# A residual stream with the model dimension on partitions, in a two-layer hybrid attention trunk

## The chip, the cores and the metric

The kernel runs on one core of one Trainium2 chip. The metric is device time in microseconds of one execution, as the median of several runs. A core has a matrix engine (TensorE, PE in the profile; PEld is its loading of weights), a vector engine (VectorE, DVE), a scalar engine (ScalarE, ACT), GpSimd (POOL) and SyncE (SP), which here only issues transfers. Each engine takes its instructions in order and waits on semaphores for the others. On-chip memory (SBUF) and the accumulators that TensorE writes (PSUM) both have 128 partitions. Transfers between SBUF and main memory (HBM) run on 16 DMA engines.

## What is computed

Two layers over x, 2048 tokens of model dimension 1024, in float32:

```python
def rms_norm(x, g):
    y = x * rsqrt(mean(x * x, axis=-1, keepdims=True) + 1e-6)
    return y * g

def even_layer(x, ...):                    # layer 0
    proj = rms_norm(x, norm_g) @ w_in      # aq, ak, av, ag, bq, bk, bv, bg
    aq, ak: rms_norm per head of 64, then rotary;  bq, bk: rms_norm per head
    ya = sliding_window_sink_attention(aq, ak, av, sinks) * silu(ag)
    yb = chunked_relbias_attention(bq, bk, bv, rel) * silu(bg)
    return x + concatenate([ya, yb]) @ w_out

def odd_layer(x, ...):                     # layer 1
    q, k, v, gate = split(rms_norm(x, norm_g) @ w_in)     # 1024 columns each
    q, k: rms_norm per head of 64, then rotary
    o = differential_attention(q1, q2, k1, k2, v, lam)    # 8 heads, values 128 wide
    return x + (rms_norm(o, subln_g) * (1 - lambda_init) * silu(gate)) @ w_out
```

## The kernel before

**Layout and precision.** Tokens are handled in four blocks (`BLK` = 512 tokens, `NB` = 4) of four tiles of 128 (`NTB`); the model dimension is eight slices (`KT`) of 128. Every float32 operand of a projection is split into a high part H, the value rounded to the type in which TensorE multiplies it fast, and a low part L, the rest. One product is three matmuls, H by H, H by L and L by H (`mm3`, lines 211 to 216). A matmul contracts over partitions, so the normed input must lie with the model dimension on partitions, while x and the residual between the layers (`self.x1`, a scratch tensor [S, D] in HBM) lie with tokens on partitions.

**Four stages.** Tile names begin with the stage: p0 (projections of layer 0), m (its attention and output projection), p1 (projections of layer 1), c (its attention, gates and output projection).

**Projection, `_project`, for both layers.** The blocks go in two halves, 3 and 2, then 1 and 0. For each block `hidden` (lines 316 to 345) takes four token tiles: it loads [128 tokens, 1024], squares and sums it on ScalarE (L325), forms the root with `rstd` (L203 to L208, two steps on ScalarE and four on VectorE), multiplies by root and norm weights on VectorE (L327), transposes eight 128x128 pieces on TensorE into PSUM (L332, tiles p0trh and p1trh), and splits them, H on ScalarE (L336) and L on VectorE (L337). In layer 1 it also stores H and L of blocks 3 to 1 (L343, L344), for the gates later. Then each group of 512 weight columns is loaded and split by `weights_by` (L303, L309 on ScalarE, L311 on GpSimd) and multiplied with both blocks. A tile of a query or key group goes through `normed` (L361 to L378): squares, sums per head, `rstd`, product, rotary on VectorE and GpSimd. After four tiles `pairs_out` (L385 to L396) transposes them and stores H and L. Value groups are copied and stored. Gate groups of layer 0 end in a sigmoid by Exp, Ln, Exp on ScalarE and a product on VectorE (L452 to L455). In layer 1 the groups are two of queries, two of keys, two of values (`cv`, L483).

`later` is a side job: `split_weights` splits weights that are needed later and stores H and L to HBM, in chunks of 512 columns. It is advanced once a group from the third group of a half on (`AHEAD` = 2); layer 1 has four chunks, two of the output weights and two of the gate weights, and they fall to groups three to six of half 0.

**Attention of layer 0, `_mix0`.** Heads go through the blocks from 3 to 0. Beside them run the last gates of the projection (`late_gate`) and, block by block, the output projection (`out_tile`): eight tiles per block, which multiply y (stationary) with the output weights (moving), add x (L505) and store to x1 (L506). Block 0's projection stands alone at the end.

**Attention of layer 1, `_mix1`.** `pace` advances scores and values of the heads, and beside them `gates` (projection of the gate columns, copied at L1088 and stored) and the output projection (`out_begin`, `out_step`, `out_end`).

**Memory.** Pools are stacked in the order in which they are opened, and layer 1's lie where layer 0's were. So the first tiles of p1 wait for the last reader of what lay there. In layer 0 the order is `big` (64 KB a partition: first the hidden blocks, then the output weights, columns 0 to 511 in its first half), `y` (36 KB: the split y), `yt`, then the rest. In layer 1 it is `hv` (32 KB), `ev` (32 KB), weights, then the others; `hidden` puts a half's first block into `ev` and its second into `hv`.

**Order.** The engines' orders are fixed when the program is built, from the order of the calls and what is ready; the calls of `weights` and of `later` alternate, and both take their staging tiles (`ws`, two in layer 1) and their w tiles (28) from the same pools.

## Time and profile before

| what | us |
|---|---|
| median of 3 runs | 2805.61 (2803.16 to 2806.72) |
| the profiled execution | 2808.08 |
| its span in the trace | 2806.3 |
| mean granted TensorE clock | 0.987 of full |
| p0: until its last matmul | 597.7 |
| m: until the end of the output projection | 1164.2 |
| p1: until its last matmul | 1757.4 |
| c: the rest | 1049 |

Rows of the profile name line, engine, operation, the tile written and those read, shapes, and after the bar the busy time, the mean duration in ns, and the engine's idle time just before with what ended it. A row of a stage gives, for a stretch of the span, the busy time and instruction count of each engine, the granted clock, the DMA engines' share and the rate in GB/s. A row of waits gives total, count and longest. "xN" counts instructions. Durations of neighbouring matmuls overlap, so their spacing is read from starts.

### The profile page before, as it was taken

How to read it: one execution, taken by the hardware profiler on the slowest of the kernel's cores; microseconds unless marked ns; L12 is line 12 of the kernel's file. 1: busy time of each engine (PE TensorE's matmuls, PEld its weight loads, DVE VectorE, ACT ScalarE, POOL GpSimd, SP SyncE). 2: the span in 40 equal slices, each digit the busy share in tenths (PEclk: the TensorE clock that was granted, in tenths of full speed). 3: DMA queues.
4: the chain of work that ended last, by engine and by line, in shares of the span. 5: the costliest groups of instructions: out<-in, count | busy, mean ns of one | idle time of the engine just before them, and what ended most of it. 6: DMA issues, size and time to landing. Idle time of an engine off the chain costs nothing.

```text
span 2806.3 us, 44052 instructions
## 1 busy us (share of the span) xinstructions
PE 2697.3 (96%) x13384; PEld 2169.2 (77%) x13384; DVE 1853.8 (66%) x4616; ACT 1606.4 (57%) x4039; POOL 1462.8 (52%) x1551
## 2 busy tenths in 40 slices
PE   7999999999899999899999999999999999999998
PEld 5888888888788888777788888777676777676776
DVE  7762285346777775598808870569886878777762
ACT  5443543367767675334334331578896787777761
POOL 3541252335545454267745670457676666767661
PEclk9999999999999999999999999999999999999999
DMA  5673343738866764666885444787868666454542
GB/s 174 225 242 140 109 142 122 232 109 239 240 179 191 201 192 132 209 217 207 253 256 192 135 136 142 239 256 219 238 190 230 183 212 200 132 183 144 166 146 83
DMA packets 356093, 521.69 MB, mean 186 GB/s; under 512 B 44816, under 2 KB 139792, under 8 KB 355856
## 3 DMA queue, kind: packets, MB, share of 16 engines
q1 hardware_dynamic: 355856, 518.87, 60.2%
q8 instruction: 107, 1.75, 0.3%
q14 instruction: 130, 1.06, 0.1%
HBM read 361.70 MB, written 157.02 MB: 185 GB/s over the span
## 4 chain that ended last, share of the span: by engine, by line
PE 77%; DVE 9%; DMA 6%; ACT 3%; issue 2%; POOL 2%; SPq 1%; DVEq 0%; ACTq 0%; POOLq 0%
PE cO L975 8%; PE p1mm L215 5%; PE p1mm L214 5%; PE p1mm L216 5%; PE cS L919 4%; PE cS L920 4%; PE ctr L971 4%; PE p0mm L214 4%; PE p0mm L216 4%; PE p0mm L215 4%; PE com L214 2%; PE com L215 2%; PE com L216 2%; PE cG L214 2%; PE mom L214 2%
## 5 line engine op out<-in xcount | busy, mean ns | idle before, releaser
L926 ACT ACTIVATE cP<-cS,cnm 128x512 f32<-128x512 f32 (+3 forms) x640 | 394.1, 621 | 138.4 <-DVE cnm L923 121.9
L923 DVE TENSOR_REDUCE cnm<-cS 128x1 f32<-128x512 f32 (+3 forms) x640 | 373.4, 600 | 52.2 <-PE cS L920 45.9
L959 POOL TENSOR_TENSOR cP<-cP,cP 128x512 f32<-128x512 f32 (+1 forms) x320 | 356.4, 1143 | 27.6 <-ACT cP L957 26.7
L958 POOL TENSOR_SCALAR cP<-cP,crl,cel 128x512 f32<-128x512 f32 (+3 forms) x288 | 210.7, 745 | 231.6 <-DVE crl L940 126.5
L214 PE MATMUL p1mm<-p1wH,p1hH 128*128 128x512 f32 x768 | 303.4, 396 | 5.5 <-ACT p1wH L309 5.5
L215 PE MATMUL p1mm<-p1wL,p1hH 128*128 128x512 f32 x768 | 304.4, 397 | 0.1
L216 PE MATMUL p1mm<-p1wH,p1hL 128*128 128x512 f32 x768 | 303.9, 396 | 0.0
L975 PE MATMUL cO<-cpt,cv 128*128 128x512 f32 (+3 forms) x640 | 288.0, 535 | 2.1 <-DVE cpt L973 2.1
L311 POOL TENSOR_TENSOR p0wL<-p0ws,p0wH 128x512 fp32r<-128x512 f32 (+1 forms) x124 | 149.7, 1238 | 267.3 <-ACT p0wH L309 263.3
L919 PE MATMUL cS<-ck,cqd 128*128 128x512 f32 (+3 forms) x640 | 265.3, 418 | 6.6 <-ACT cP L926 6.0
L973 DVE COPY cpt<-ctr 128x512 f32<-128x512 f32 (+1 forms) x320 | 191.0, 604 | 107.3 <-PE ctr L971 104.1
L214 PE MATMUL p0mm<-p0wH,p0hH 128*128 128x512 f32 (+1 forms) x640 | 238.5, 374 | 7.0 <-ACT p0vt L473 4.7
L216 PE MATMUL p0mm<-p0wH,p0hL 128*128 128x512 f32 (+1 forms) x640 | 238.3, 373 | 2.0 <-DVE p0hL L337 1.9
L215 PE MATMUL p0mm<-p0wL,p0hH 128*128 128x512 f32 (+1 forms) x640 | 238.4, 373 | 0.0
L311 POOL TENSOR_TENSOR p1wL<-p1ws,p1wH 128x512 fp32r<-128x512 f32 x128 | 167.2, 1327 | 124.6 <-ACT p1wH L309 118.5
L920 PE MATMUL cS<-ck,cql 128*128 128x512 f32 (+3 forms) x640 | 232.0, 367 | 0.0
L971 PEld LDWEIGHTS ctr<-ident,cP 128*128 128x128 f32 x1088 | 138.7, 142 | 115.4 <-issue 62.3
L957 ACT ACTIVATE cP<-cP,cc 128x512 f32<-128x512 f32 (+1 forms) x320 | 189.2, 651 | 18.2 <-DVE cc L943 17.7
L971 PE MATMUL ctr<-ident,cP 128*128 128x128 f32 x1088 | 177.1, 275 | 1.8 <-POOL cP L959 1.5
L214 PEld LDWEIGHTS p1mm<-p1wH,p1hH 128*128 128x128 f32 x768 | 145.8, 190 | 34.6 <-ACT p1wH L309 5.7
L215 PEld LDWEIGHTS p1mm<-p1wL,p1hH 128*128 128x128 f32 x768 | 145.6, 190 | 29.9 <-POOL p1wL L311 0.9
L216 PEld LDWEIGHTS p1mm<-p1wH,p1hL 128*128 128x128 f32 x768 | 145.8, 190 | 28.9 <-issue 0.2
(301 smaller groups left out, 7046.9 us busy)
## 6 DMA issues: line engine op xcount, KB each, us to landing
p1ws<-in_od_w_in_dram SPq DMA_DIRECT2D x56, 512.0 KB, 4.3
p0ws<-in_ev_w_in_dram SPq DMA_DIRECT2D x48, 512.0 KB, 4.2
ck<-kH SPq DMA_DIRECT2D x144, 128.0 KB, 3.4
ck<-kL SPq DMA_DIRECT2D x144, 128.0 KB, 3.5
cv<-v SPq DMA_DIRECT2D x72, 256.0 KB, 4.0
cqd<-qH SPq DMA_DIRECT2D x128, 128.0 KB, 4.6
cql<-qL SPq DMA_DIRECT2D x128, 128.0 KB, 4.7
cwH<-wgH SPq DMA_DIRECT2D x64, 256.0 KB, 5.1
```

The costliest lines, as they stand in the source:

```text
L214: mm(ps, aH, bH, start=first, stop=False)
L215: mm(ps, aH, bL, start=False, stop=False)
L216: mm(ps, aL, bH, start=False, stop=last)
L311: low.tensor_tensor(l[:, :width], ws[:, k, :width], f32(h[:, :width]), ALU.subtract)
L919: mm(ps, qd[:, m, js], kt[:, :wd], start=True, stop=False)
L920: self.anchor = mm(ps, ql[:, m, js], kt[:, :wd], start=False, stop=True).ins
L923: nc.vector.tensor_reduce(nm[:, m, z:z + 1], ps, AX.X, ALU.max, negate=True)
L926: exp = nc.scalar.activation(chunks[z][:, :wd], ps, AF.Exp, bias=nm[:, m, z:z + 1], accum_out=acc).ins
L958: nc.gpsimd.tensor_scalar(p1, p1, rl[:, 0:1], e1, ALU.mult, ALU.mult)
L959: nc.gpsimd.tensor_tensor(p1, p1, p2, ALU.add)
L971: nc.tensor.transpose(tp[:, (j - j0) * P:(j - j0 + 1) * P], us[j][kt // 4][:, kk:kk + P], self.ident)
L975: mm(O[:, j0 * P:], v, T[:, :wd], start=(kt == 0), stop=(kt == nkt - 1), skip_group_check=True)
```

## The change

1. x is given to the kernel, and taken from it, with the model dimension first: x, x1 and the output are [D, S] in HBM. The transposition of both ends is in the host's layout code.
2. `hidden` loads slices [128 of the model dimension, 512 tokens], multiplies by the norm weight per partition while it splits (H on ScalarE, L on VectorE), and no longer applies the root. No transposes.
3. The root per token is applied behind the projection: in layer 0 the squares are summed over slices on GpSimd (`squares`), in layer 1 they are taken and summed in `out_tile` of layer 0. `roots` sums over partitions with one-column matmuls, forms the root as a column per token tile (`rcol`), eps times the mean square (`ecol`), and by four transposes the root as a row over all partitions (`row`). Queries and keys need only the eps term, since their own norm cancels the root; values are scaled by the column while they are copied; gates are multiplied by the row.
4. `out_tile` and the output projection of layer 1 swap stationary and moving operand.
5. Around it, mostly in layer 1: the first value group comes first, tables are formed behind it; `normed` takes two tiles at a time, with one of the two rotary sums on VectorE; `pairs_out` is called later (`turn`); the first group of half 0 is issued slice by slice over four PSUM tiles (`project_tiles`); half 1 takes block 0 first; `hidden` exchanges `hv` and `ev`, and the pools' order changes; low parts of later weights are formed on VectorE, two chunks in the last group of half 0 and two in the first of half 1; value tiles are stored from ScalarE's queue. In the attention of layer 1 a query is loaded by four transfers instead of eight, and pools are reordered.

```diff
+    def squares(self, layer, b, sq, first):
+        nc, parts = self.nc, list(sq)
+        if first:
+            self.row[layer][b] = self.rows.tile([P, BLK], F32, tag="row", name=f"row{layer}")
+            if len(parts) > 1:
+                nc.gpsimd.tensor_tensor(self.row[layer][b], parts.pop(0), parts.pop(0), ALU.add)
+        for part in parts:
+            nc.gpsimd.tensor_tensor(self.row[layer][b], self.row[layer][b], part, ALU.add)
+
+    def roots(self, layer, b, sm, sb, ptr):
...
+        for j in range(NTB):
+            nc.tensor.matmul(ps[:, j:j + 1], row[:, j * P:(j + 1) * P], f32(self.ones[:, 0:1]), start=True, stop=True)
+        ms = sm.tile([P, NTB], F32, tag="xms", name=n + "ms")
+        nc.vector.tensor_scalar(ms, ps[:, :NTB], 1.0 / D, EPS, ALU.mult, ALU.add)
+        self.rstd(sm, ms, NTB, "x", r)
+        nc.vector.tensor_scalar(e, ms, EPS, None, ALU.mult)
...
+        for j in range(NTB):
+            js = slice(j * P, (j + 1) * P)
+            nc.scalar.activation(wide[:, js], f32(self.ones), AF.Copy, scale=r[:, j:j + 1])
+            nc.tensor.transpose(ps[:, js], wide[:, js], self.ident)
+        nc.scalar.activation(row, ps, AF.Copy)
+        self.col[layer][b] = r, e
...
         def hidden_tile(part, i):
-            pl, tag = (self.big, "w") if layer == 0 else (self.hv, "h") if i else (ev, "v")
+            pl, tag = (self.big, "w") if layer == 0 else (ev, "v") if i else (self.hv, "h")
...
+            values = [("cv", 2048 + 512 * i, 512, dict(c0=512 * i)) for i in range(2)]
+            groups = values[:1] + groups + values[1:]
...
-                    low = nc.vector if first and k else nc.gpsimd
+                    low = nc.vector if k >= 2 - vector else nc.gpsimd
...
         def hidden(b, i, between=()):
...
+            for q in range(4):
+                xt = xp.tile([P, 2, BLK], F32, tag="xt", name=n + "xt")
+                for i in range(2):
+                    k = 2 * q + i
+                    nc.sync.dma_start(xt[:, i, :], x[k * P:(k + 1) * P, tok])
+                    g = self.norm[layer][:, k:k + 1]
+                    nc.scalar.activation(hH[:, k, :], xt[:, i, :], AF.Copy, scale=g)
+                    nc.vector.scalar_tensor_tensor(hL[:, k, :], xt[:, i, :], g, f32(hH[:, k, :]), ALU.mult, ALU.subtract)
+                if layer == 0:
+                    sq = xp.tile([P, 2, BLK], F32, tag="vb", name=n + "xq", bufs=2)
+                    nc.scalar.activation(sq, xt, AF.Square)
+                    self.squares(0, b, (sq[:, 0, :], sq[:, 1, :]), q == 0)
                 next(between, None)
...
+            self.roots(layer, b, sm, sb, ptr)
...
-                wH, wL = weights(c0 + 512 * i, 512, W)
+                wH, wL = weights(c0 + 512 * i, 512, W, 2 * layer)
...
-                if gi >= self.AHEAD:
+                for _ in range(gi >= self.AHEAD if layer == 0 else 2 * ((half, gi) in ((0, 5), (1, 0)))):
                     next(ahead, None)
...
-                            nc.scalar.activation(gt, ps, AF.Exp, scale=-1.0)
-                            nc.scalar.activation(gt, gt, AF.Ln, bias=self.one)
-                            nc.scalar.activation(gt, gt, AF.Exp, scale=-1.0)
-                            nc.vector.tensor_tensor(gt, ps, gt, ALU.mult)
+                            nc.vector.tensor_tensor(gt, ps, self.row[0][b], ALU.mult)
+                            nc.scalar.activation(sg, gt, AF.Exp, scale=-1.0)
+                            nc.scalar.activation(sg, sg, AF.Ln, bias=self.one)
+                            nc.scalar.activation(sg, sg, AF.Exp, scale=-1.0)
+                            nc.gpsimd.tensor_tensor(gt, gt, sg, ALU.mult)
...
+                            nc.scalar.activation(vt, ps, AF.Copy, scale=rc)
+                            nc.scalar.dma_start(s["v"][tok, o["c0"]:o["c0"] + 512], vt)
...
+            self.mm3(ps, w[0][k][c][:, js], w[1][k][c][:, js], *y[k], i == 0, i == KT - 1, self.anchor)
...
+        if (j, c) == (0, 0):
+            self.squares(1, b, (), True)
+            nc.scalar.activation(self.row[1][b], xr, AF.Square)
+        else:
+            sq = sb.tile([P, BLK], F32, tag="xq", name=n + "xq", bufs=1)
+            nc.scalar.activation(sq, xr, AF.Square)
+            self.squares(1, b, (sq,), False)
...
-                    nc.scalar.activation(gt, ps, AF.Copy)
+                    nc.vector.tensor_tensor(gt, ps, self.row[1][b], ALU.mult)
```

More of the change, by code (lines that the diff above doesn't have):

```diff
@@ new lines, in project_tiles @@
+        def project_tiles(h, w, width, outside):
+            pss = [pmm.tile([P, 512], F32, tag="mm", name=n + "mm") for _ in range(NTB)]
+            steps = [(k, j) for k in range(outside) for j in range(NTB)]
+            steps += [(k, j) for j in range(NTB) for k in range(outside, KT)]
+            for k, j in steps:
+                self.mm3(
+                    pss[j][:, :width], h[0][:, k, j * P:(j + 1) * P], h[1][:, k, j * P:(j + 1) * P],
+                    w[0][k][:, :width], w[1][k][:, :width], k == 0, k == KT - 1,
+                )
+                if k == KT - 1:
+                    yield pss[j]
@@ L419, in _project, with turn @@
         ahead = later()
+        turned = []
+        def turn():
+            while turned:
+                pairs_out(*turned.pop(0))
         for half in range(2):
             blocks = (NB - 1 - 2 * half, NB - 2 - 2 * half)
+            if layer == 1 and half == 1:
+                blocks = blocks[::-1]
             ready = None
@@ L424, in _project @@
                 ready = [], []
-                by = weights_by(groups[0][1], groups[0][2], W, *ready, first=True)
+                by = weights_by(groups[0][1], groups[0][2], W, *ready, vector=1)
                 next(by)
@@ L460, in _project @@
                     xs = []
+                    tiles = project_tiles(h[bi], w, width, 4) if layer == half == gi == bi == 0 else None
                     for j in range(NTB):
@@ new lines, in _project, with out_tile @@
+                        if layer == 0:
+                            turn()
+                if not tabs:
+                    tables()
+            turn()
+    def out_tile(self, y, w, j, b, c, xin, xout, sb, pmm, n, tag, order=range(KT), after=None):
+        nc = self.nc
+        js, tok = slice(j * P, (j + 1) * P), slice(b * BLK, (b + 1) * BLK)
+        cs = slice(c * 512 + j * P, c * 512 + (j + 1) * P)
+        xr = sb.tile([P, BLK], F32, tag="xr", name=n + "xr", bufs=2)
+        nc.sync.dma_start(xr, xin[cs, tok])
+        ps = pmm.tile([P, BLK], F32, tag=tag, name=n + "om")
```

233 lines of the change are left out of this document (116 added, 117 removed).

## The prediction

> **What bounds the kernel now.** I read the page first, then busy time by stage, then who waited for whom on TensorE.
>
> ```profile
> span 2806.3 us, 44052 instructions
> ## 1 busy us (share of the span) xinstructions
> PE 2697.3 (96%) x13384; PEld 2169.2 (77%) x13384; DVE 1853.8 (66%) x4616; ACT 1606.4 (57%) x4039; POOL 1462.8 (52%) x1551
> ```
> ```profile
> core 0: us, PE busy (x) PEld busy (x) DVE busy (x) ACT busy (x) POOL busy (x), PEclk, DMA share, GB/s
> 0.00:60.00 60.00, 40.75 (x189) 32.01 (x190) 49.76 (x112) 32.38 (x77) 20.90 (x22) 0.98 0.56 171
> ...
> 0.00:600.00 600.00, 572.58 (x2845) 479.73 (x2845) 317.61 (x696) 261.26 (x591) 208.93 (x203) 1.00 0.51 167
> 600.00:1120.00 520.00, 493.18 (x3073) 432.76 (x3073) 375.65 (x1260) 370.28 (x984) 256.68 (x386) 0.99 0.69 195
> ...
> 1164.00:1758.00 594.00, 576.58 (x2680) 474.41 (x2678) 390.72 (x681) 220.67 (x496) 331.43 (x256) 0.98 0.60 196
> 1758.00:2806.00 1048.00, 1014.33 (x4606) 748.79 (x4605) 757.32 (x1952) 746.86 (x1953) 663.25 (x704) 0.98 0.62 188
> ```
> ```profile
> 1165.00:1275.00 110.00, 98.38 (x455) 80.43 (x456) 102.20 (x185) 49.33 (x119) 62.19 (x48) 0.94 0.62 217
> ```
>
> The reader is to see TensorE busy for 96% of the span, so nearly everything gained must be TensorE work taken away or a gap closed. Gaps are concentrated: the first 60 us (19 us idle) and the opening of the second layer's projections, where VectorE is busy 102 of 110 us and the granted clock falls to 0.94. The rows of single waits name the cause:
>
> ```profile
> PE p0trh L332 <- DVE p0xt L327: 13.7, 3, 13.1
> ...
> PE p1trq L385 <- DVE p1eL L391: 7.2, 3, 2.9
> ...
> PE p1mm L214 <- ACT p1wH L309: 5.5, 1, 5.5
> ```
>
> **Token transposes removed, both layers.** 256 fp32 transposes (tiles p0trh, p1trh) go.
>
> ```profile
> L332 PE MATMUL p1trh<-ident,p1xt 128*128 128x128 f32 x128 | 17.9, 283 | 3.8 <-DVE p1q8u L206 3.5 <-DVE p1xt L327 0.3
> L332 PE MATMUL p0trh<-ident,p0xt 128*128 128x128 f32 x128 | 17.8, 283 | 15.6 <-DVE p0xt L327 13.7 <-DVE p0hL L337 1.9
> ```
> ```profile
> 37.09 1.04 PE L332 MATMUL p0trh<-ident,p0xt 128*128 128x128 f32 x8
> ...
> 1755.13 0.39 PE L215 MATMUL p1mm<-p1wL,p1hH 128*128 128x512 f32 x1
> ...
> 1757.40 0.39 PE L216 MATMUL p1mm<-p1wH,p1hL 128*128 128x512 f32 x1
> ```
>
> From these, dense spacings: ten projection matmuls in 2.27 us, 0.2275 us each; eight transposes in 1.04 us, the last lasting 0.28, so 0.109 us each inside a run. Added are the `roots`: per block four one-column matmuls and four transposes, eight blocks. The nearest row is the removed transpose at 17.8/128 = 0.14 us; 8 x 0.14 = 1.1 us per block, 4.5 us per layer.
>
> **Start of layer 0.** Today's projections in the first 60 us:
>
> ```profile
> 0.00:60.00 60.00, 33.64 (x129) 24.77 (x130) 2.73 (x4) 2.98 (x5) 0.98 0.56 171
> ```
> ```profile
> 6.89 1.15 ACT L309 ACTIVATE p0wH<-p0ws 128x512 fp32r<-128x512 f32 x2 [4.56 <-DMA p0ws<-in_ev_w_in_dram]
> ...
> 8.26 1.06 ACT L325 ACTIVATE p0junk<-p0xt 128x1024 f32<-128x1024 f32 x1 [0.22 <-DMA p0xt<-in_x_dram]
> ```
>
> The first row is tile p0mm alone: 129 matmuls. Afterwards the first token tile needs all eight slices of the block, not one token tile of x, so it starts no earlier: ScalarE must do eight weight copies (8 x 0.575), eight copies of x at about the same price (4.6) and three double squares (3 x 1.06) from 6.9 us on, ending at 19.3; with the low part and three matmuls I put that tile's end at 21 us. From there TensorE can run dense: (60 - 21)/0.2275 = 171 matmuls, less about 18 for pair transposes and roots, plus the tile's 24 make 177, 48 more than now, 10.9 us. ScalarE stays nearly full for the second block, so I take 9 (bounds 4 to 12). In the second half of layer 0, half of the p0trh row (8.9 us) goes and roots (2.2) come: I take 6. Layer 0: **-15** (bounds -8 to -20). The 24 gate products added to GpSimd and its row sums lie in a stage where it is busy 209 of 600 us in all. A qk root now waits for its block's token root; behind it on VectorE queue further tiles' steps, for which TensorE's four PSUM tiles (24 x 0.2275 = 5.5 us of matmuls each) are the cover. What is late next there is the key/value group's chain on VectorE and ScalarE, unchanged.
>
> **Second layer's projections.** From the row 1164 to 1758: 2304 matmuls x 0.2275 = 524 us, 256 pair transposes x 0.109 = 28, together 552 of 594. The other 42 are token transposes (some 12), waits, and half-speed clock behind the waits. What takes VectorE off: squares and per-token root leave `hidden`, the qk root runs once per two tiles, value columns come first, tables move behind them.
>
> ```profile
> L207 DVE TENSOR_TENSOR p1q8u<-p1q8u,p1q8ms 128x8 f32<-128x8 f32 x26 | 22.4, 860 | 0.7
> ...
> 10.20 0.16 DVE L207 TENSOR_TENSOR p0xu<-p0xu,p0xms 128x1 f32<-128x1 f32 x1
> ```
>
> The first row is the window 1165 to 1360: a root step takes 860 ns there, against 160 alone at 10 us, so halving these steps saves more than their width says. The opening wait (5.5 us) goes as well: x copies land in the two slots whose output weights are read out halfway through the last output projection, and weight tiles lie behind the y tiles. What is late next is the matmul itself. I leave 4 us of waits and 4.5 of roots: 42 - 8.5 = 33.5, **-34** with transposes issued before 1164.
>
> [...]
>
> **Later weights: what the quicker stage collides with.** Today four chunks of later weights (`split_weights`) are spread over four groups. Afterwards two go into the last value group of half 0 and two into the first of half 1, each 8 x 24 x 0.2275 = 43.7 us long. Loads of the next group's weights stand behind them, as now:
>
> ```profile
> 1343.21 0.41 SPq L303 DMA_DIRECT2D p1ws<-in_od_w_out_dram  x1
> ...
> 1347.05 0.45 SPq L303 DMA_DIRECT2D p1ws<-in_od_w_in_dram  x1
> ```
> ```profile
> v<-p1v SPq DMA_DIRECT2D x31, 256.0 KB, 3.2
> ...
> hH<-p1hH SPq DMA_DIRECT2D x3, 2048.0 KB, 8.7
> ...
> p1ws<-in_od_w_out_dram SPq DMA_DIRECT2D x8, 512.0 KB, 4.1
> wo1H<-p1wH SPq DMA_DIRECT2D x16, 256.0 KB, 3.2
> ```
> ```profile
> DMA  9999989999999999999996926086479314000230
> ...
> q1 hardware_dynamic: 11715, 10.46, 75.7%
> ```
> ```profile
> 1180.00:1200.00 20.00, 19.68 (x99) 16.10 (x98) 18.32 (x39) 11.20 (x30) 9.58 (x8) 1.00 1.00 374
> ```
>
> The second fence gives the sizes; eight value tiles of 256 KB, or one block of next weights, are 2.1 MB, hH and hL of a block 4.2. The third is 1429 to 1473, the value group with one chunk: DMA is full for 25 us, 10.7 us are free. A chunk is 4 x 512 KB in and 16 x 256 KB out, 6.3 MB. The first group gains a chunk and a block of x1 (2.1 MB): 8.4 MB at 374 GB/s, 22.4 us, 11.7 late. The second holds two chunks, next weights, x1, value stores (2.1 each) and hH and hL, 23.1 MB, 61.8 us, 18.1 late. For 11.2 us of this, the value stores (moved to ScalarE's queue), nobody waits: **+19**. Bounds: 0, if what is queued first covers it; and with all 44.1 MB of both groups (2.1 of it the last k stores) in the way at that value group's own rate, 10.46 MB in 44 us over its share 0.757, 314 GB/s, 140 - 87 = 53.
>
> **Attention of layer 0.** Each of 32 output tiles adds a square on ScalarE, 28 a sum on GpSimd.
>
> ```profile
> L999 POOL TENSOR_TENSOR cot<-cot,cgg 128x512 f32<-128x512 f32 x32 | 41.5, 1297 | 60.7 <-ACT csq L995 50.6 <-DMA cgg<-g 9.9
> ...
> L995 ACT ACTIVATE csq<-cot 128x512 f32<-128x512 f32 x32 | 20.4, 637 | 0.2
> ...
> L1088 ACT ACTIVATE cgt<-cG 128x512 f32<-128x512 f32 x32 | 19.0, 594 | 15.2 <-PE cG L216 12.1 <-DMA p1hH<-hH 3.0
> ...
> L455 DVE TENSOR_TENSOR p0gt<-p0mg,p0gt 128x512 f32<-128x512 f32 x24 | 16.6, 691 | 97.8 <-ACT p0gt L454 97.8
> ```
>
> 28 x 1.3 = 36 us on GpSimd (257 of 520 busy) and 32 x 0.64 = 20 on ScalarE (370 of 520). The square's buffer is single, so a square waits for GpSimd's last sum, and behind it in ScalarE's queue stand the exponentials the score tiles wait for. TensorE idles 27 us here; raised by GpSimd's 14% that is **+4** (bounds 0 and 36, every sum exposed).
>
> **Attention of layer 1.** The 32 gate copies (0.59 us) leave ScalarE; VectorE gains 32 products, at the 0.69 us of L455. 128 query load issues go from SP's queue, bytes unchanged. Both engines are 71% busy: **0** (bounds -4 and +6).
>
> **Sum.** The profiled execution took 2808.08 us (span 2806.3 and 1.8 around it), 2.5 above the median. 2808.1 - 15 - 34 + 19 + 4 = 2782.1, less 2.5: **2780 us**.
>
> **Rivals.** (a) *Later weights stay hidden.* For: 10.7 us are free in that group, and two staged slices of weights can be loaded ahead. Then +19 becomes 0: 2761. (b) *Squares hold ScalarE in layer 0's attention.* If each of 28 waits one sum of 1.3 us and half of the 36 us reaches TensorE, 18 instead of 4: 2794. Against: output tiles come one in 16 us. (c) *DMA saturates in the two value groups*, the mechanism on the other side: price 53 us instead of 19, 2814, slower. It decides from 50 us late, a rate under 44.1 MB/137 us = 321 GB/s; above that and up to 333 GB/s it ends within 0.2% of before. For: the group already reaches share 1.00 with one chunk. Against: without that group's small packets the row 1180 to 1200 reached 374.
> [...]
> (d) *It doesn't do what it says*: 256 transposes go but 32 wide ones and 32 small matmuls come; counted.
>
> **How the numbers follow.** Forecast 0.45, (a) 0.25, (b) 0.08, (c) 0.22, half of it slower and half within 0.2%, about what a measurement of this kernel can tell from no change. Faster: 0.45 + 0.25 + 0.08 = 0.78. The range 2752 to 2808 takes (a) with layer 0 and the waits at their good ends, and (c) to where it equals before; a tenth is left out on each side.
>
> **What would show it.** Right: no trh rows; the first 60 us with some 175 p0mm matmuls; no wait of p1mm at the stage's opening; VectorE well under 90% behind it; p1mm waiting for p1wH at the end of half 0 and one group on, some 10 us each, with DMA share near 1.00. Wrong: those waits absent (a) or over 20 us each (c); TensorE's idle time from 600 to 1120 up by more than 10 us (b); layer 0's first tile ending after 27 us.

## The result and the profile after

After the change the kernel takes 2881.57 us in the median (2877.17 to 2884.66, 4 runs), before it 2806.16 (2803.16 to 2807.89, 4 runs on the same chip): ratio 1.0269, 95% interval 1.0251 to 1.0287, some 75 us slower. The forecast was 2780, with a range of 2752 to 2808.

The head of the page of the changed kernel:

```profile
span 2875.4 us, 43341 instructions
...
PE 2698.1 (94%) x13224; PEld 2164.3 (75%) x13224; DVE 1873.8 (65%) x4520; ACT 1591.8 (55%) x3911; POOL 1495.1 (52%) x1567
```

The transposes are gone, yet TensorE is busy as long as before (2697.3), and its idle time rose from 109 to 177 us. Busy time by stage shows where; the stages are cut at the end of the last p0mg, mom and p1mm matmul. First the kernel before, then the changed one (columns as in the prediction's rows):

```profile
0.00:598.10 598.10, 571.11 (x2834) 478.46 (x2835) 316.56 (x691) 259.43 (x589) 208.12 (x203) 1.00 0.51 167
598.10:1164.30 566.20, 535.63 (x3272) 467.72 (x3270) 389.20 (x1293) 379.48 (x1004) 260.06 (x389) 0.99 0.68 192
1164.30:1757.80 593.50, 576.08 (x2677) 474.07 (x2675) 390.71 (x681) 220.53 (x495) 331.43 (x256) 0.98 0.60 196
1757.80:2806.30 1048.50, 1014.53 (x4608) 748.99 (x4607) 757.32 (x1952) 746.99 (x1953) 663.25 (x704) 0.98 0.62 188
```
```profile
0.00:619.20 619.20, 573.75 (x2752) 478.11 (x2752) 328.79 (x647) 263.76 (x568) 276.99 (x244) 0.97 0.46 152
619.20:1209.10 589.90, 539.38 (x3264) 468.76 (x3264) 389.97 (x1285) 393.67 (x1026) 313.82 (x440) 0.97 0.74 195
1209.10:1813.40 604.30, 566.15 (x2603) 469.11 (x2603) 376.41 (x604) 199.94 (x397) 243.15 (x180) 0.97 0.59 190
1813.40:2875.40 1062.00, 1018.81 (x4608) 748.28 (x4607) 778.62 (x1984) 734.45 (x1921) 661.13 (x704) 0.98 0.64 185
```

All four stages are longer: p0 by 21.1 us, m by 23.7, p1 by 10.8, c by 13.5, together 69.1. In p0 TensorE's busy time rose by 2.6 us although transposes left; the granted clock there fell from 1.00 to 0.97. The longest waits of TensorE in the changed kernel (total, count, longest):

```profile
PE p1mm L251 <- ACT p1wH L342: 26.6, 2, 17.9
PE n0rr L244 <- ACT n0wide L243: 15.0, 3, 11.2
...
PE mSA L673 <- DMA mksA<-akL: 12.1, 1, 12.1
...
PE n1rr L244 <- ACT n1wide L243: 5.4, 2, 5.1
```

Each of the first three belongs to one place. **The opening of p0**, TensorE, then VectorE, then ScalarE, in order of time:

```profile
26.59 0.50 PE L253 MATMUL p0mm<-p0wH,p0hL 128*128 128x512 f32 x1 [1.84 <-DVE p0hL L360]
...
37.21 0.39 PE L253 MATMUL p0mm<-p0wH,p0hL 128*128 128x512 f32 x1
48.81 1.36 PE L244 MATMUL n0rr<-ident,n0wide 128*128 128x128 f32 x4 [11.21 <-ACT n0wide L243]
...
59.54 0.76 PE L251 MATMUL p0mm<-p0wH,p0hH 128*128 128x512 f32 x1 [4.77 <-DVE p0q8r L215]
```
```profile
37.63 3.42 DVE L360 SCALAR_TENSOR_TENSOR p0hL<-p0xt,norm,p0hH 128x512 fp32r<-128x512 f32 x2
40.97 0.15 DVE L236 TENSOR_SCALAR n0ms<-n0ss 128x4 f32<-128x4 f32 x1
...
43.78 4.08 DVE L360 SCALAR_TENSOR_TENSOR p0hL<-p0xt,norm,p0hH 128x512 fp32r<-128x512 f32 x3
...
48.16 0.16 DVE L215 SCALAR_TENSOR_TENSOR rcol<-xu,xy 128x4 f32<-128x4 f32 x1
```
```profile
48.35 1.28 ACT L243 ACTIVATE n0wide<-ones,rcol 128x128 f32<-128x128 f32 x4 [5.34 <-DVE rcol L215]
...
52.96 1.28 ACT L243 ACTIVATE n0wide<-ones,rcol 128x128 f32<-128x128 f32 x4 [0.62 <-DVE rcol L215]
54.15 0.57 ACT L400 ACTIVATE p0sq<-p0mm 128x512 f32<-128x512 f32 x1
```

The first four token tiles are multiplied by 37.6 us. Their four PSUM tiles are released only behind the query root. That root's first step, p0sq, stands on ScalarE behind the wide copies of both blocks' token roots, and the steps of these roots stand on VectorE among the low parts of the second block. From 37.6 to 59.5 us no projection matmul runs. The first matmul into the fifth tile, here at 59.5 us, is what most experiments on p0 below are read by.

**The opening of m.** SyncE's queue, first before, then after the change:

```profile
579.09 17.93 SPq L456 DMA_DIRECT2D g<-p0gt  x4
598.91 0.45 SPq L548 DMA_DIRECT2D mqd<-bqH  x1
```
```profile
585.29 38.42 SPq L518 DMA_DIRECT2D g<-p0gt  x8
623.82 0.37 SPq L655 DMA_DIRECT2D mfar<-in_relfar_dram  x1
624.25 0.46 SPq L632 DMA_DIRECT2D mqd<-aqH  x1
```

Before, the first head's loads had been issued long ago (the mqd at 598.91 is a later head's, and the first score ran at 597.88); now the stage's very first load comes behind the last gate's store, 5 us after the last p0 matmul, and TensorE waits 12.1 us.

**The seam of p1's halves**, two windows of the changed kernel:

```profile
1490.00:1511.00 21.00, 12.36 (x60) 10.28 (x58) 6.28 (x11) 8.48 (x15) 0.00 (x0) 0.86 1.04 367
1559.00:1577.00 18.00, 0.48 (x3) 0.06 (x1) 3.88 (x6) 4.32 (x8) 0.00 (x0) 0.61 1.09 342
```

In the second window every engine stands nearly idle, in the first TensorE stops at 1502 us, and in both the DMA engines are full. These are the waits for p1wH, 8.7 and 17.9 us, at the places that the prediction named.

### The profile page after: what moved, and what is told of

The parts are those of the page before. It is cut to its first block, busy times and chain, and to the rows that moved or that the text cites. A ratio compares the mean times of both kernels' runs of the same rounds, so it can differ in the third digit from the quotient of the medians.

```text
span 2875.4 us, 43341 instructions
## 1 busy us (share of the span) xinstructions
PE 2698.1 (94%) x13224; PEld 2164.3 (75%) x13224; DVE 1873.8 (65%) x4520; ACT 1591.8 (55%) x3911; POOL 1495.1 (52%) x1567
## 3 DMA queue, kind: packets, MB, share of 16 engines
q14 instruction: 128, 1.04, 0.1%
## 4 chain that ended last, share of the span: by engine, by line
PE 74%; DMA 10%; DVE 8%; ACT 3%; issue 3%; POOL 2%; SPq 1%; ACTq 0%; DVEq 0%; POOLq 0%
PE cO L1060 8%; PE p1mm L251 5%; PE p1mm L252 5%; PE p1mm L253 5%; PE cS L1004 4%; PE cS L1005 4%; PE ctr L1056 4%; PE p0mm L251 3%; PE p0mm L252 3%; PE p0mm L253 3%; PE com L251 2%; PE com L252 2%; PE com L253 2%; PE mtrB L830 2%; PE cG L251 2%
## 5 line engine op out<-in xcount | busy, mean ns | idle before, releaser
L251 PE MATMUL p1mm<-p1wH,p1hH 128*128 128x512 f32 x768 | 302.7, 399 | 31.9 <-ACT p1wH L342 26.6
L1004 PE MATMUL cS<-ck,cqd 128*128 128x512 f32 (+3 forms) x640 | 265.5, 419 | 11.3 <-ACT cP L1011 10.6
L344 POOL TENSOR_TENSOR p1wL<-p1ws,p1wH 128x512 fp32r<-128x512 f32 x96 | 132.5, 1402 | 178.5 <-ACT p1wH L342 128.8
L251 PEld LDWEIGHTS p1mm<-p1wH,p1hH 128*128 128x128 f32 x768 | 146.8, 191 | 63.1 <-ACT p1wH L342 27.1
L252 PEld LDWEIGHTS p1mm<-p1wL,p1hH 128*128 128x128 f32 x768 | 146.2, 190 | 29.3
```

Of the source, the lines that this page charges most:

```text
L251: mm(ps, aH, bH, start=first, stop=False)
L252: mm(ps, aH, bL, start=False, stop=False)
L344: low.tensor_tensor(l[:, :width], ws[:, k, :width], f32(h[:, :width]), ALU.subtract)
L1004: mm(ps, qd[:, m, js], kt[:, :wd], start=True, stop=False)
```

## Experiments

Every kernel is the changed one with the edit given; "the mends" are the edits of e1_spread and e6_row and a memory of its own for sg together. Stage lengths in us, each from one execution, from the same cuts. In kernels whose edits leave a stage alone, p0 took 618.6 to 620.9 us, p1 603.0 to 607.6, m 584.6 to 593.2 and c 1059.4 to 1070.4; smaller differences than these ranges show nothing. Times are single runs, for e9, e10, e16, e17 and e18 medians; the kernel before, run beside them, took 2799.0 to 2811.4 us.

| kernel | p0 | m | p1 | c | time |
|---|---|---|---|---|---|
| before | 598.1 | 566.2 | 593.5 | 1048.5 | 2806.2 |
| changed | 619.2 | 589.9 | 604.3 | 1062.0 | 2881.6 |
| e1_spread | 620.5 | 586.5 | 580.7 | 1066.7 | 2856.6 |
| e2_sg | 632.4 | 571.3 | 607.3 | 1063.5 | 2876.4 |
| e3b_roots | 625.1 | 593.2 | 605.8 | 1064.1 | 2890.4 |
| e4_gact | 618.7 | 590.0 | 603.3 | 1062.4 | 2876.2 |
| e5_c | 618.6 | 572.8 | 605.2 | 1063.5 | 2862.0 |
| e6_row | 608.0 | 587.3 | 596.7 | 1059.4 | 2853.3 |
| e7_order | 623.0 | 584.6 | 606.1 | 1068.7 | 2884.2 |
| e8_nosq | 618.9 | 568.6 | 603.0 | 1066.3 | 2858.6 |
| e9_mended | 610.3 | 570.5 | 573.1 | 1064.3 | 2825.7 |
| e10_pesum | 612.1 | 573.5 | 575.4 | 1067.1 | 2831.0 |
| e11_cplain | 619.1 | 586.2 | 607.2 | 1065.3 | 2879.6 |
| e12_swapc | 620.9 | 584.6 | 607.6 | 1069.1 | 2884.0 |
| e13_eps | 607.7 | 568.5 | 575.5 | 1063.8 | 2817.3 |
| e14_p1old | 619.6 | 589.8 | 598.4 | 1066.8 | 2876.8 |
| e15_bq | 619.8 | 568.1 | 573.5 | 1070.4 | 2834.0 |
| e16_ones | 605.1 | 573.8 | 574.7 | 1067.6 | 2819.1 |
| e17_tab | 601.8 | 569.3 | 574.5 | 1065.2 | 2812.7 |
| e18_old | 601.5 | 579.3 | 589.0 | 1062.3 | 2830.9 |

### Later weights spread again (e1_spread)

```diff
-for _ in range(gi >= self.AHEAD if layer == 0 else 2 * ((half, gi) in ((0, 5), (1, 0)))):
+for _ in range(gi >= self.AHEAD):
```


> The changed kernel, but with layer 1's later weights put back one chunk per group (groups three to six of half 0) in place of two chunks in each of the two value groups at the seam. Theory: the two waits of p1mm for p1wH, 8.7 and 17.9 us, and the half-speed clock behind each come from 44 MB of transfers in those two groups. Expected: both waits gone, the stage p1 (from the end of the output projection to its last projection matmul) 604 us before this edit and about 570 to 577 behind it, the whole 2843 to 2852 us. Rival: the transfers only move, and other groups wait for p1wH instead: p1 stays within 8 us of 604 and the whole above 2865.

p1 took 580.7 us, 23.6 less, and no wait for p1wH is left. The crowding is shown; p1 without it is 12.8 us shorter than before the change. Both lengths missed what was expected by some 4 us (570 to 577, and 2843 to 2852 for the whole). In p1 TensorE still idles 18.2 us, most of it at three places:

```profile
PE p1trq L433 <- POOL p1xn L426: 6.2, 6, 1.2
PE n1rr L244 <- ACT n1wide L243: 6.1, 1, 6.1
PE p1mm L251 <- ACT p1hH L359: 4.5, 1, 4.5
```

The pair transposes (p1trq) wait for GpSimd's rotary sums, the transposes of the root's row (n1rr) for the wide copies, and the opening for the first split of x1.

### The gates' scratch moved (e2_sg, then own memory in e5_c)

```diff
-sg = sb.tile([P, 512], F32, tag="t2", name=n + "sg")
+sg = xp.tile([P, 2 * BLK], F32, tag="vb", name=n + "sg", bufs=2)[:, :512]
```


> The changed kernel, but the new scratch tile of layer 0's gates (sg, under the tag t2 of the pool sb) lies in the pool xp under the tag vb. Theory: the tag t2 lies at the bottom of the memory that the next stage's load tiles take over, so that the loads that open layer 0's attention can only be issued once the last gate is multiplied, and the 12.1 us wait of mSA for mksA is this. Expected: the first mqd load issued before the last matmul of p0, that wait under 2 us, the stretch from the last p0mg matmul to the last mom matmul 590 us without this edit and 573 to 579 with it, the whole 2859 to 2868 us. Rival: the loads stand behind the gates' stores in SyncE's queue only because of the order, whatever the memory: the wait stays at 10 to 13 us.

SyncE's queue of this run:

```profile
561.75 0.45 SPq L632 DMA_DIRECT2D mqd<-aqH  x1
```

The stage's first query load is issued 70 us before p0 ends, the wait is gone and m is 571.3 us. So it was memory. By the order of the pools m's load tiles lie where sb's t2 lies; t2 had been free since the rotary groups, and sg kept it in use to the end. The gain was lost in p0, 13.2 us longer: vb also holds the squares of x, and in the second half these now stand behind the gates (the first at 350 us instead of 332). With a tag of its own (`tag="sg"`, in e5_c below) p0 is back at 618.6 and m at 572.8.

### The squares of x1 (e8_nosq)

```diff
-nc.scalar.activation(self.row[1][b], xr, AF.Square)
+nc.scalar.activation(self.row[1][b], xr, AF.Square, scale=math.sqrt(8.0))
...
-nc.scalar.activation(sq, xr, AF.Square)
-self.squares(1, b, (sq,), False)
+pass
```


> The changed kernel with sg in memory of its own (as in the first run of this call), and with seven of eight squares and all sums of x1 left out in layer 0's output tiles (the root of layer 1 then comes from one eighth of the model dimension, its square times eight). Theory: those squares and sums are what is left of the lengthening of layer 0's attention, 571 us without the wait at its opening against 566 before the change. Expected: 565 to 568 us. Rival: they are hidden, and it stays at 570 or above.

The kernel that it starts from, with sg in memory of its own, is e5_c. m took 568.6 us against 572.8 there, just outside what was expected. But seven kernels that keep the squares and the sums and have sg in memory of its own took 568.1 to 573.8 us in m (e5_c, e9, e10, e13, e15, e16, e17), so these 4 us are not resolved: squares and sums cost little, and how much isn't shown.

### The opening of p0 (e3b_roots, e6_row, e7_order)

```diff
+    with tc.issue_after(behind) if behind is not None else nullcontext():     # behind: the first block's token root
         nc.vector.scalar_tensor_tensor(hL[:, k, :], xt[:, i, :], g, f32(hH[:, k, :]), ALU.mult, ALU.subtract)
...
+if not (layer == 0 and b == NB - 2):
+    self.roots(layer, b, sm, sb, ptr)
...
+if layer == half == gi == bi == 0:
+    self.roots(0, blocks[1], sm, sb, ptr)
```


> The changed kernel, but the low parts of the second block of x are queued on VectorE behind the first block's token root, and the second block's root is formed behind the first block's first group. Theory: TensorE's idle time from 37 to 60 us is VectorE's in-order queue: the root's steps stand behind the tables and the next block's low parts, four PSUM tiles are held by the queries that wait for the root, and the wide copies for the root's row keep TensorE's queue shut. Expected: n0wide's wait under 4 us instead of 11.2, p0mm again at 45 to 50 us instead of 59.5, the stage p0 (to the last p0mg matmul) 605 to 611 us instead of 618.8, the whole 2866 to 2872. Rival: the GpSimd row sums, which end at 26 us for the first block and 47 for the second, are the limit: p0mm starts again no earlier than 56 us and p0 stays above 615.

n0wide's wait fell to 2.9 us, but the fifth PSUM tile came at 52.3 us and p0 took 625.1: the low parts of the second block still stood ahead of the queries' steps on VectorE, and 7.9 us were lost from 80 to 88 us, where the second block's queries waited for a root formed only at 75 to 76 us. The expected 605 to 611 us were missed, on the rival's side (above 615); moving one link was not enough.

```diff
+if gi == (5 if layer == 0 else 2):
+    for b in blocks:
+        self.root_row(layer, b, sb, ptr)     # wide copies, transposes, copy: out of roots()
```


> The changed kernel, but the root's row (wide copies, four transposes, copy) is no longer formed with the root's column: in layer 0 it is formed ahead of the first gate group, in layer 1 ahead of the third group of a half. Theory: the transposes n0rr and n1rr, which nobody needs before the gates, stand in TensorE's in-order queue and cost their waits (15.0 us in p0, 5.4 in p1) and the half-speed clock behind them. Expected: those waits under 2 us together, p0 603 to 608 us instead of 618.8, p1 595 to 600 instead of 604.3. Rival: the queue is shut anyway, because four PSUM tiles are held until the queries' root is formed, which stands behind both blocks' token roots on VectorE and ScalarE: p0mm waits for p0q8r or p0xn in their place, p0 is above 613.

p0 608.0, p1 596.7: both as expected, 11.2 and 7.6 us less, with no wait for the row's transposes left. But the rival holds in part: the queue stays shut until 51.7 us, now by the column's matmuls, which wait for GpSimd's sums, and then by the queries' product p0xn.

```profile
47.09 1.23 PE L234 MATMUL n0ss<-ones,row 128*128 128x1 f32 x5 [9.18 <-POOL row L226]
51.73 0.77 PE L255 MATMUL p0mm<-p0wH,p0hH 128*128 128x512 f32 x1 [2.77 <-DVE p0xn L418]
```

```diff
 for bi, b in turns:
+    if len(h) <= bi:
+        h.append(hidden(blocks[1], 1))
```


> The changed kernel, but the second block of x of layer 0's first half is handled behind the first block's first group (in the order of the calls). Theory: the squares and roots of the first block's query tiles stand behind the second block's x, its squares and its root on ScalarE and VectorE, so that TensorE's four PSUM tiles are held until 59.5 us; with the order turned they are free by 45 to 50 us. Expected: first matmul of the fifth PSUM tile at 45 to 50 us, p0 605 to 611 us instead of 618.8. Rival: what is gained there is lost behind it, because the second block's split now comes late and TensorE waits for p0hH or p0hL: p0 within 4 us of 618.8.

Fifth tile at 54.8 us, p0 623.0, both outside what was expected. What the order gained was lost from 83 to 91 us, as the rival said, though not in a wait for the second block's split: TensorE waited there 7.8 us for a step of the queries' root (p0q8u) on VectorE.

### The mends together, and what is left of p0 (e9, e10, e13, e15, e16, e17)

> The changed kernel with three mends that were tried alone before: later weights one chunk per group, sg in memory of its own, the root's row formed ahead of the gates. Theory: their gains lie in different stages and add: p0 608 us, layer 0's attention 572, p1 604 - 24 - 8 = 572 to 575, the last stage 1060 to 1066; the whole 2812 to 2822 us, still slower than before the change by 0.3 to 0.7%. Rival: each only uncovers the next wait at its place: above 2830.

Ratio to before 1.0059 (1.0040 to 1.0078). Stage by stage the gains add: 8.9, 19.4 and 31.2 us in p0, m and p1, against 11.2, 17.1 and 31.2 from the single edits. The median, 2825.7 us, is above the 2812 to 2822 that were expected and below the rival's 2830. Left in p0's opening is a wait of 9.2 us for GpSimd's sums.

```diff
-self.squares(0, b, (sq[:, 0, :], sq[:, 1, :]), q == 0)
+for i in range(2):
+    for j in range(NTB):
+        nc.tensor.matmul(self.sums[:, j:j + 1], sq[:, i, j * P:(j + 1) * P], f32(self.ones[:, 0:1]), ...)
```


> The kernel of the first run of this call, but for the first two blocks of layer 0 the squares are summed over slices by 32 one-column matmuls per block on TensorE in place of GpSimd's adds. Theory: what is left of the idle time of p0's opening is that the first groups' PSUM tiles wait for the token root, which waits for GpSimd's sums (they end at 26 and 47 us), and that VectorE's low parts take 1.4 to 1.75 us beside GpSimd's adds against 0.74 alone. Expected: low parts of x under 1.0 us in the mean, the fifth PSUM tile's first matmul before 46 us, p0 595 to 602 us against 608, the whole 7 to 12 us below the first run of this call. Rival: loads of x and ScalarE are the limit: p0 within 4 us of 608, or above it by the 6.4 us that 64 matmuls cost at 0.1 us.

The kernel that it starts from, and the "first run" of its expectation, is e9_mended. Low parts of x in the first 60 us, without GpSimd's adds, then with them (e9_mended, and the changed kernel):

```profile
L367 DVE SCALAR_TENSOR_TENSOR p0hL<-p0xt,norm,p0hH 128x512 fp32r<-128x512 f32 x16 | 11.3, 741 | 1.4 <-ACT p0hH L366 1.4
```
```profile
L364 DVE SCALAR_TENSOR_TENSOR p0hL<-p0xt,norm,p0hH 128x512 fp32r<-128x512 f32 x16 | 18.9, 1207 | 0.0
```
```profile
L360 DVE SCALAR_TENSOR_TENSOR p0hL<-p0xt,norm,p0hH 128x512 fp32r<-128x512 f32 x16 | 22.9, 1467 | 0.0
```

and TensorE in e10_pesum:

```profile
30.00:60.00 30.00, 29.29 (x125) 24.76 (x126) 18.46 (x43) 13.36 (x26) 5.97 (x6) 0.69 0.40 134
...
45.10 0.40 PE L258 MATMUL p0mm<-p0wH,p0hH 128*128 128x512 f32 x1
45.33 4.02 PE L377 MATMUL n0ss<-ones,p0xq 128*128 128x1 f32 x32
49.21 0.77 PE L259 MATMUL p0mm<-p0wL,p0hH 128*128 128x512 f32 x1
49.78 0.63 PE L260 MATMUL p0mm<-p0wH,p0hL 128*128 128x512 f32 x1
```

The waits are gone, the low parts 39% shorter, the fifth tile comes at 39.9 us, and yet p0 is 612.1 where 595 to 602 were expected: TensorE is 18.7 us longer busy than in e9_mended, with the sums (128 records, two per matmul, 16.9 us in all) and with matmuls at half speed behind them, at a granted clock of 0.50 from 40.0 to 44.7 and from 49.3 to 54.9 us (ratio to before 1.0079, 1.0058 to 1.0100). The theory on the wait holds; my price for the sums was wrong, 0.26 us for a one-column matmul and not 0.1.

The next two are the mends with one more edit each.

```diff
+if layer == 0 and t // NTB >= NB - 2 and not self.rooted0:      # the first group; the roots are formed behind it
+    nc.vector.tensor_scalar(to, to, 1.0 / HD, EPS, ALU.mult, ALU.add)
+    continue
+e = self.col[layer][t // NTB][1]
 nc.vector.tensor_scalar(to, to, 1.0 / HD, e[:, t % NTB:t % NTB + 1], ALU.mult, ALU.add)
```

> The three mends together, and in layer 0's first group the eps term of the queries' norm is a constant in place of eps times the mean square (left out: the token root's part in these 16 tiles' norm), so that both blocks' roots are formed behind that group. Theory: what is left of p0's lengthening (610 us with the mends against 598 before the change) is that the first group's PSUM tiles are held until the token roots are there. Expected: fifth PSUM tile's first matmul at 40 to 45 us instead of 52.7, p0 598 to 602 us. Rival: VectorE itself is full there (29.8 of 30 us busy from 30 to 60 us, low parts of x at 1.2 us each beside GpSimd's adds), so that the tiles come free hardly earlier: fifth tile after 48 us, p0 605 or more.

Fifth tile at 51.0 us, p0 607.7, as the rival said: it isn't the token root alone. VectorE was busy 29.4 us of 30 to 60.

```diff
 groups = [
+    ("qk", 1280, 512, dict(tab=None, gain=True, dH="bqH", dL="bqL", p0=0)),
+    ("qk", 1792, 512, dict(tab=None, dH="bkH", dL="bkL", p0=0)),
     ("qk", 0, 512, dict(tab="q", dH="aqH", dL="aqL", p0=0)),
     ("akv", 512, 256, dict(tab="k", dH="akH", dL="akL", p0=0)),
-    ("qk", 1280, 512, dict(tab=None, gain=True, dH="bqH", dL="bqL", p0=0)),
-    ("qk", 1792, 512, dict(tab=None, dH="bkH", dL="bkL", p0=0)),
```


> The three mends together, and layer 0's groups begin with the two of the chunked attention, which have no rotary, so that the tables are formed behind the first group. Theory: VectorE bounds p0's opening (30 to 60 us: 29.8 of 30 busy); some 10 us of table building and the rotary products leave it. Expected: fifth PSUM tile's first matmul at 42 to 46 us instead of 52.7, p0 600 to 604 us instead of 610, the whole 2806 to 2814 us. Rival: GpSimd's sums for the second block (until 47 us) hold the queue all the same: fifth tile after 50 us, p0 above 606.

Fifth tile at 49.0 us though VectorE was busy only 21.8 of those 30 us; p0 619.8, with 7.0 and 7.8 us lost in waits for the copies of value tiles (p0vt). It isn't VectorE's load alone either: in its queue the queries' steps stand among the second block's low parts, the last of which ends at 44.6 us.

```diff
+sums = ptr.tile([P, 512], F32, tag="tr", name="n0sum")
+nc.tensor.matmul(sums, self.ones, sq[:, i, :], start=(q == i == 0), stop=(q == 3 and i == 1))
...
+h.append(hidden(blocks[1], 1))              # this and the lines below in e17_tab alone
 if layer == 0 and not tabs:
     tables()
-h.append(hidden(blocks[1], 1))
```


> The three mends together, and for the first two blocks of layer 0 the squares are summed on TensorE by 512-wide matmuls with the ones as stationary operand, eight per block (the sum stands on every partition), in place of GpSimd's adds. Theory: the one-column sums tried before did take the waits away (TensorE busy 29.3 of 30 us from 30 to 60) but cost TensorE some 18 us themselves and let its clock fall; 16 wide matmuls cost 3.6 us at 0.2275 and keep the clock. Expected: fifth PSUM tile's first matmul at 38 to 43 us, clock above 0.9 from 30 to 60 us, p0 596 to 601 us against 610 with the mends alone and 598 before the change, the whole 2804 to 2812 us, within 0.3% of before. Rival: loads of the second block's x, which are issued behind the parameters' loads from 23 us on, are the limit: p0 above 605.

> The kernel of the first run of this call, with the parameters and tables formed behind the second block's x in place of ahead of it. Theory: some twenty small loads stand ahead of the second block's x in SyncE's queue and its scratch takes one of three x buffers; without them the second block's slices come earlier. Expected: p0 2 to 6 us below the first run of this call. Rival: the first group's rotary then waits for the tables and holds PSUM: p0 equal or up to 6 us longer.

e17_tab starts from e16_ones, the "first run" of its expectation. In e16_ones p0 took 605.1 us, the fifth tile came at 45.7 us and the clock from 30 to 60 us was 0.83: p0, tile, clock and the whole, 2819.1, all missed what was expected, and p0 just meets the rival's bound. In e17_tab p0 took 601.8. Ratios to before: 1.0046 (1.0030 to 1.0063) and 1.0030 (1.0016 to 1.0043). The second block's loads may bind, for 3.3 us, little more than p0 differs between kernels that leave it alone. Of p0's 21.1 us, 17.4 are given back.

### The last stage (e4, e5, e11, e12, e14, e18)

```diff
-nc.vector.tensor_tensor(gt, ps, self.row[1][b], ALU.mult)
+nc.scalar.activation(gt, ps, AF.Copy, scale=0.03)
```


> The changed kernel, but layer 1's gates leave PSUM by a ScalarE copy with a constant scale of 0.03: the product with the token root's row is left out. Theory: the 32 products on VectorE are what lengthens the last stage, 1062 us against 1049 before the change (cG waits 3.5 us for them, and cnm stands behind them). Expected: the last stage 1052 to 1056 us. Rival: it comes from elsewhere (larger query loads, the pools' order, the place at which half-speed clock falls): 1060 us or more.

```diff
-for part, q in (("qH", qd), ("qL", ql)):
-    both = s[part][h, :, tok].rearrange("(m r) t -> r m t", m=2)
...
+for m in range(2):
+    for part, q in (("qH", qd), ("qL", ql)):
+        nc.sync.dma_start(f32(q[0:HD, m, :]), s[part][h, r, tok])
+        nc.sync.dma_start(f32(q[HD:P, m, :]), s[part][h, r, tok])
```


> The changed kernel with two edits in stages that do not touch: the gates' scratch of layer 0 (sg) gets a tag and memory of its own at the end of the pool xp, and layer 1's attention gets back the order of its pools and the eight loads per query that it had before the change; the products on VectorE and the swapped operands stay. Theory for the first: as the earlier run with sg elsewhere, the wait that opens layer 0's attention goes (that stage 571 us instead of 590), and, since sg no longer shares a buffer with the squares of x, p0 stays at 617 to 621 us instead of the 632 of that run. Theory for the second: the order of the pools or the larger query loads make the last stage long; expected 1048 to 1053 us instead of 1062. Rival: the last stage stays at 1060 or above, so that it is neither.

e4_gact and the second edit of e5_c together:

> The changed kernel with all of layer 1's attention as it was before the change, except the swapped operands of its output projection: gates copied by ScalarE (constant scale of 0.03, the root's row left out), pools in the old order, eight loads per query. Theory: each of the two edits alone leaves the last stage at 1062 to 1064 us, but together they bring it back: 1048 to 1053. Rival: it stays above 1058; then its length comes from the swapped operands or from what the stage before leaves behind (order of the queues, place of the hidden block, blocks in the other order).

```diff
-self.mm3(ps, *(t[:, js] for t in w[k]), *y[b][k], k == 0, k == KT - 1, self.anchor)
+self.mm3(ps, *(t[:, js] for t in y[b][k]), *w[k], k == 0, k == KT - 1, self.anchor)
```


> The changed kernel, but in layer 1's output projection y is the stationary operand again, as before the change (the output tiles are then written as [tokens, model dimension] into places that are laid out the other way, and x1 is added untransposed). Theory: the swap costs the last stage its 13 us: 1050 us instead of 1062. Rival: stationary and moving have the same shapes and the same spacing either way: 1060 or more.

```diff
-groups = values[:1] + groups + values[1:]
+groups += values
...
-self.last_hidden = h[0]
+self.last_hidden = h[1]
...
-nc.scalar.dma_start(s["v"][tok, o["c0"]:o["c0"] + 512], vt)
+nc.sync.dma_start(s["v"][tok, o["c0"]:o["c0"] + 512], vt)
```


> The changed kernel with layer 1's projections in the old order: query and key groups first and both value groups last, block 1 before block 0 in the second half, the hidden blocks in hv and ev as before the change, value tiles stored from SyncE's queue, tables ahead of the groups. Theory: the last stage's 13 us come from what the projections leave at its opening (the last values just stored, the gates' hidden block in other memory). Expected: the last stage 1048 to 1054 us instead of 1062. Rival: it stays above 1058, then the length lies in the last stage's own order and the cause stays open.

The last run joins e17_tab, e14_p1old (weights spread) and e5_c:

> The best kernel so far (mends, wide sums on TensorE, tables behind the second block's x), and in it both halves of what was so far undone one at a time for the last stage: layer 1's projections in the old order with the old order of pools (values last, block 1 before block 0, hidden blocks and value stores as before the change), and layer 1's attention with the old order of pools and eight loads per query. The gates' products on VectorE and the swapped operands stay. Theory: old pools behind the new projections, or new ones behind the old, each wait at the seam; only both together give back what the last stage had: 1048 to 1054 us instead of 1062 to 1067, and, with the projections at 575 to 585 us, the whole 2797 to 2810 us. Rival: the last stage stays at 1058 or above: neither memory nor the order of the stage before is its cause, and it stays open.

1062.4, 1063.5, 1065.3, 1069.1, 1066.8 and 1062.3 us: six times the rival. None of these edits, alone or in these combinations, gives the 13 us back; over all changed kernels the stage took 1059 to 1070 us, before the change 1048.5. In the waits the 9 us of added idle time are spread (cS for cP 10.6 us in place of 6.0, cG for the gates' products 3.5, cS for cql 2.5, and against them cG for its weights 5.8 in place of 10.9); that the 4.3 us of added busy time are half-speed matmuls behind them isn't shown. e18 also lost 10 us in m and 14.5 in p1 against e17_tab (ratio to before 1.0079, 1.0052 to 1.0106).

The length of the stage hides one thing that the traces show. Counted from the stage's start, the 250th score matmul (cS) comes 9.9 us later in the changed kernel than before, but in e18_old only 2.3 us later; at the 325th the two are level again, 7.4 and 7.1 us late. So the old pools and the old order together did bring the stage's opening back, as e18_old's theory had it, and something behind it took the gain away. In both, some 5 us more are lost between the 1000th and the 1200th. No run undoes all edits at once, and the late calls of `pairs_out` are undone in none. The cause stays open.

## Why the prediction was wrong

| step | forecast | measured |
|---|---|---|
| p0 | -15 | +21.1 |
| m: squares and sums | +4 | not resolved, small (e5_c, e8_nosq) |
| m: its opening | not seen | about +17 (changed less e5_c) |
| p1 without crowding | -34 | -12.8 (e1_spread) |
| p1: later weights crowding | +19 | +23.6 (changed less e1_spread) |
| c | 0 | +13.5, open |

**p0: the step "From there TensorE can run dense" failed.** I had named the new wait, a query root behind its block's token root, and took four PSUM tiles as its cover, worth 22 us of matmuls. But the opening spends these tiles first. It fills all four by 37.6 us, and until then it is ahead of the kernel before, with 96 matmuls against 72 (p0mm alone, first before, then after):

```profile
0.00:37.60 37.60, 18.27 (x72) 13.33 (x72) 0.00 (x0) 1.49 (x3) 1.00 0.70 210
```
```profile
0.00:37.60 37.60, 27.24 (x96) 20.85 (x96) 0.00 (x0) 0.00 (x0) 0.95 0.70 205
```

Then nothing is left to multiply into, and the root chain (squares, GpSimd's sums, one-column matmuls, VectorE's steps behind tables and the next block's low parts, wide copies) ends long after. I priced the `roots` by their instructions, 4.5 us a layer, and not by the queues they close. Of the signs, the row of p0mm for the first 60 us,

```profile
0.00:60.00 60.00, 27.70 (x97) 21.33 (x98) 0.68 (x1) 2.25 (x4) 0.81 0.57 171
```

shows 97 matmuls instead of 175, at a clock of 0.81. The first token tile ended at 27.1 us, at the bound given for wrong, and here too the wrong engine was priced:

```profile
17.48 1.38 ACT L359 ACTIVATE p0hH<-p0xt,norm 128x512 fp32r<-128x512 f32 x2 [0.38 <-DMA p0xt<-in_x_dram]
```
```profile
24.79 1.75 DVE L360 SCALAR_TENSOR_TENSOR p0hL<-p0xt,norm,p0hH 128x512 fp32r<-128x512 f32 x1
```

ScalarE copied the eighth slice by 18.9 us, close to the 19.3 of the prediction, but VectorE ended its low part only at 26.5 us, behind the parameters' steps. The 16 low parts of the first 60 us took VectorE 22.9 us, and 11.3 where TensorE sums in GpSimd's place (e10_pesum); the forecast has no term for this. The row of the root was half of the loss (e6_row); summing on TensorE (e16 against e9) gave back another 5.2 us, and moving the parameters and tables (e17) 3.3.

**m: I looked at a small term and missed the large one beside it.** The prediction counted the gates' new products as work on an idle GpSimd. It didn't ask where the new scratch tile lies, nor which transfers stand behind the last gate's store. For the squares and sums it named a wait, but took the size from GpSimd's added 14% without a working; if +4 is right, that is luck. Rival (b), +18, is refuted: the idle time rose by 20 us, but in the seven kernels with the opening mended m is 2 to 8 us longer than before.

**p1: the mechanism of the crowding was right**, in place and in size (26.6 us of waits at DMA shares of 1.04 and 1.09; measured 23.6 against 19, a difference no larger than p1's range between kernels that leave it alone; 342 to 367 GB/s went through, not 374). **Mis-sized was the -34.** It left 4 us of waits; without crowding (e1_spread) 18.2 remain. "The opening wait (5.5 us) goes as well" failed: the wait is 4.7 us, and it isn't for x1, whose loads had been issued at 1169 us. The first split starts only at the end of the output projection; in e9_mended the trace names its last matmul as the releaser:

```profile
1180.85 3.78 ACT L363 ACTIVATE p1hH<-p1xt,norm 128x512 fp32r<-128x512 f32 x6 [1.18 <-PE mom L257]
```

"What is late next is the matmul itself" failed too: next are the root's row (its wait 5.4 us, the stage 7.6 us shorter in e6_row) and the pair transposes behind GpSimd's rotary sums (6.2 us in e1_spread). With spread weights and the row out of the way the stage is 573.1 us, 20.4 below before. VectorE well under 90% came true at the stage's opening, 53.4 of the first 110 us against 102.2 before, but TensorE's idle time there only fell from 11.6 to 8.9 us.

**Rival (c)** pointed to the slower side by the crowding alone, at 2814. Without crowding (e1_spread) the kernel is still 57.6 us slower than before (2856.6 against 2799.0, single runs side by side): the sign comes from the openings of p0 and m and from c, to which I gave no rival.

**The sum** was made of prices of instructions where the changed kernel pays for order. No version tried beats the kernel before; the best one timed repeatedly, e17_tab, is 0.30% slower, with c's lengthening unexplained.

## What to carry to other kernels

When a factor is moved behind a matmul, price the time from the last input of that factor to the release of the first PSUM tile that needs it, not the instructions: at this stage's opening nothing covered it, and whatever of it isn't needed at once (here the root's row) belongs behind the first group. A new scratch tile in a tag that had gone quiet can keep the memory of the next stage's loads in use; ask of every such tag who lies on it next. And spread side traffic by the bytes per group that fit beside the group's own.

## What the runs showed of the hardware

TensorE's granted clock was about half of full behind the long waits of p1. In the kernel before, behind the 5.5 us wait for p1wH, it was 0.52 from 1169.9 to 1173.5 us and 1.00 from 1173.5 to 1180. In the changed kernel it was 0.51 from 1511.0 to 1515.4 us, behind the 8.7 us wait, and 0.50 from 1577.4 to 1583.1, behind the 17.9 us wait; from 1583.6 to 1589 us it was 1.00 again. The window from 1559 us, nearly all idle, shows 0.61. At 0.50 the 512-wide matmuls took 0.63 us and started 0.43 us apart, at 1.00 they took 0.39 and started 0.23 apart.

It fell to half also behind stretches in which TensorE was busy by the profile, but with one-column matmuls only. In e10_pesum TensorE ran 29.3 of the 30 us from 30 to 60 us and was granted 0.69. From 45.3 to 49.2 us it ran one-column matmuls; behind these 4.0 us, with no idle time between, 512-wide matmuls took 0.63 us where the one just ahead of them had taken 0.40, and from 49.3 to 54.9 us the clock was 0.50. In e10_pesum, runs of one-column matmuls were followed by half speed as the waits above are.

VectorE's low parts of x took longer beside GpSimd's adds. The 16 of the first 60 us took 1467 ns in the mean in the changed kernel and 1207 in e9_mended, and 741 in e10_pesum, where TensorE sums in GpSimd's place. In e13_eps GpSimd was busy from 30.5 to 46.8 us: two low parts that start at 42.7 us took 3.02 us together, and the two that start at 46.8 and 48.0 us took 0.74 each. It isn't so for every one: in the changed kernel the low part at 22.76 us took 0.74 us while GpSimd added.
